# A decoder trunk on one core: the last tiles' transposes move into the first up product, the norm vectors into other tiles, and three groups of small work to other places in the queues

## The chip, the cores and the metric

One core of one Trainium2 chip runs the whole program; the other cores are idle. The metric is device microseconds from launch to the end, as the median of several runs. The profile is of one execution, and a span in it is the time from the first to the last instruction.

## What is computed

Two layers over 512 tokens of 1024 features, in float32. Layer 0 is a latent attention, layer 1 a banded one (window 128) whose keys and values come from the input of that layer. Each mixer and each MLP is followed by a scaled residual and a layer norm. Cut to what matters here:

```python
x = _layernorm(alpha * x + y, ln_mix_g[l], ln_mix_b[l])                    # y: the mixer
x = _layernorm(alpha * x + _mlp(x, mlp_w_up[l], mlp_w_down[l]), ln_mlp_g[l], ln_mlp_b[l])

def _mlp(x, w_up, w_down):          # 1024 -> 4096 -> 1024
    h = jax.nn.relu(x @ w_up)
    return (h * h) @ w_down
```

## The kernel before

**Numbers in two halves.** Every float32 operand is split into a rounded high part and the rest: ScalarE (ACT) writes the high part with a copy, VectorE (DVE) subtracts it (`split`, lines 75 to 83). A product is three matmuls, high by high, high by low and low by high (`three`). GpSimd (POOL) does the subtraction for some weights, and issues the adding DMAs.

**Tiles.** Tokens are in four tiles of 128 (t = 0 to 3). After a mixer, `TokMajor.finish` makes the second half of the output columns tile by tile, 24 matmuls of 512 columns for each t; as soon as a tile's group is in PSUM, DVE adds the residual (`add_scaled`, L541), takes the statistics (L534), and `layer_norm` (from L395) applies L400, L403 and L407, with a power on POOL (L384) between. `turn` then transposes the normed tile on TensorE (PE) through two PSUM banks of their own, and ACT and DVE split it into the operand of the next product. `finish` turns tile t-1 behind the groups of t = 1 and 2, so tiles 0 and 1; tiles 2 and 3 are turned later, by whoever comes next.

**MLP.** Up and down products are done with seven products in place of eight (U1 to U7 and D1 to D7, sums of quarter blocks). The order of the first ones is written out by hand: U1 U2 U5 U3 U6 U7 U4 D1 D2 (`FIRST_STEPS`). One U is four groups j = 0 to 3 of 12 matmuls of 256 columns. U1 and U2 need tiles 0 and 1 alone; U5 needs all four. U1 turns tile 2 behind its group j = 1, and U2 turns tile 3 behind its j = 1. D1 needs the factor f1, which is relu squared of the quarter a11, which is whole after U6; the quarters a21 and a22 are whole after U7 and U4.

**Weights** come from one stream in the order of use. `prep` of an entry issues the loading DMA on SP's queue, into one of two `raw` tiles (or a `wq` tile that later entries add to), and the split into one of four pairs of `wh` and `wl`. U1's and U2's four weights have places of their own (`w_fac`, `w_quada`, `w_quadb`, `w_a`). `hold` says up to which entry the stream may run ahead, and `prepare(n)` lets it run n further; `early`, the last argument of `finish`, says after which tile's norm it does.

**Band attention.** `begin` (from L560) makes keys and first queries in two halves of 256 tokens: chunks k0, k1 and sq0, each into a PSUM bank and evicted at once by 64-row copies (L1151, L1152, L1196, L1197); tile 2 is turned behind k1, tile 3 behind sq0.

**Order.** PE and SP run in program order. The other engines run in the order that the scheduler set when the program was built; `high_priority`, `pin` (program order) and `behind` / `issue_after` (an instruction may not stand ahead of a named one on its engine) steer it.

Of the kernel before, what the change touches and what calls it, by code (L numbers as in the profile page):

```python
# [15 lines left out]
P = 128  # L16
# [32 lines left out]
def build(tc, nc, io, out):  # L49
    with ExitStack() as top:  # L50
# [76 lines left out]
        def queue(name, ap, low=nc.vector):  # L127
# [24 lines left out]
            off_ring.append(False)  # L152
# [12 lines left out]
        def queue_seven(name, key, chunk):  # L165
# [88 lines left out]
        def mlp_stream(l):  # L254
            holds.append(len(stream) + 4)
# [22 lines left out]
        for m in range(2):  # L278
            queue("w_k", io["w_k"][m])
        for m in range(8):  # L280
# [109 lines left out]
        def load_gb(g, b):  # L390
            gb = gp.tile([P, 2, D], F32, tag="gb", bufs=1, name=nm("gb"))
            pe(nc.sync.dma_start(gb[:, 0, :], g.partition_broadcast(P)))
            pe(nc.sync.dma_start(gb[:, 1, :], b.partition_broadcast(P)))
            return gb

        def layer_norm(t, gb, dst):
# [6 lines left out]
            pin(nc.vector.scalar_tensor_tensor(x, x, mv[:, 0:1], gb[:, 0, :], ALU.subtract, ALU.mult))  # L403
            n = 2 if dst is None and t == NT - 1 else 1
            for i in range(n):
                c = slice(i * D // n, (i + 1) * D // n)
                pin(nc.vector.scalar_tensor_tensor(x[:, c], x[:, c], r, gb[:, 1, c], ALU.mult, ALU.add))  # L407
                if dst is None:
                    nc.sync.dma_start(out[t * P : (t + 1) * P, c], x[:, c])

        def turn_tokens(t, dst):

            tk = slice(t * P, (t + 1) * P)
            for n in range(2):
# [4 lines left out]
                split(dst.hs[n][:, :, tk], dst.ls[n][:, :, tk], pt)  # L419
# [140 lines left out]
        def begin(src, chunks):  # L560


            ws = [weights(name) for name, _ in chunks]
            for half_ in range(2):
                cols = slice(half_ * 256, half_ * 256 + 256)
                for i, (_, evac) in enumerate(chunks):
                    b = bank(256)
                    feat_major(src, ws[i], b, cols)
                    evac(cols, b)
                    if half_ == 0 and i > 0:  # L570
                        with tc.high_priority():
                            src.turn(i + 1)

# [86 lines left out]
        def mlp(src, gb, dst, mp):  # L660
# [17 lines left out]
            class Block:  # L678
# [18 lines left out]
                def up(self, n):  # L697
# [5 lines left out]
                    for j in range(4):  # L703
# [12 lines left out]
                        if (self.q, j) == (0, 1) and n in (1, 2):  # L716
                            with tc.high_priority():
                                src.turn(n + 1)

                def up_out(self, n, i):  # L720
# [7 lines left out]
                    elif n == 2:  # L728
                        nc.scalar.activation(self.quarter("a12")[:, pairs], of(1), AF.Relu)
                        if i == 1:  # L730
                            with behind(state.pop("s4") if self.q == 0 else None):
                                nc.scalar.activation(self.g["a12"], self.g["a12"], AF.Square)
# [18 lines left out]
                def factor(self, n, quad=False):  # L751
# [5 lines left out]
                    split(f[:, 0], f[:, 1], g[2] if n == 0 else self.down.sum(n, *g))  # L757
# [36 lines left out]
            for i, (which, q, n) in enumerate(steps):  # L794
                if which == "D":
# [3 lines left out]
                    at.setdefault(max(min(i - 2, i_last), i_q), []).append((q, n))  # L799
# [31 lines left out]
            TokMajor(Hidden(), add_last, "down").finish(gb, dst)  # L831
# [300 lines left out]
        gb = lambda: load_gb(io["ln_mix_g"][0], io["ln_mix_b"][0])  # L1132
        x2 = Feat()
        with tc.tile_pool(name="mlp0", bufs=1) as mp:
# [3 lines left out]
            proj.finish(gb, x1, (0, 0, 0, 2))  # L1138
            mlp(x1, lambda: load_gb(io["ln_mlp_g"][0], io["ln_mlp_b"][0]), x2, mp)
# [3 lines left out]
        with tc.tile_pool(name="swa", bufs=1) as mp:  # L1143
# [145 lines left out]
            for m in range(1, 8):  # L1289
                for part in range(2):  # L1290
                    fill.append((2.6, 2 * m - AHEAD_B - 3 + part, -9, lambda m=m, part=part: queries(m, part)))
                if m == 1:
# [4 lines left out]
            load_bias(0)  # L1297
# [3 lines left out]
                + [("w_sq", lambda cols, b: query_parts(0, cols, b))],  # L1301
# [4 lines left out]
        gb = lambda: load_gb(io["ln_mix_g"][1], io["ln_mix_b"][1])  # L1306
        with tc.tile_pool(name="mlp1", bufs=1) as mp:
# [3 lines left out]
            proj.finish(gb, x3, (0, 0, 0, 2))  # L1311
            mlp(x3, lambda: load_gb(io["ln_mlp_g"][1], io["ln_mlp_b"][1]), None, mp)
# [109 lines left out]
```

## Time and profile before

| | us |
|---|---|
| median of 3 runs (lowest, highest) | 1033.54 (1028.98, 1035.62) |
| the profiled execution's own time | 1032.31 |
| its span | 1030.4 |
| PE busy in it | 998.7 (97%) |
| DVE, ACT, POOL busy | 769.6 (75%), 556.3 (54%), 218.5 (21%) |
| HBM traffic | 146 GB/s over the span |

A busy PE is read with care here: a matmul's row lasts longer than the distance to the next one, so what PE loses is read from the starts of successive matmuls, not from the busy share. Times in the prediction are microseconds from the start of the span.

### The profile page before, as it was taken

How to read it: one execution, taken by the hardware profiler on the slowest of the kernel's cores; microseconds unless marked ns; L12 is line 12 of the kernel's file. 1: busy time of each engine (PE TensorE's matmuls, PEld its weight loads, DVE VectorE, ACT ScalarE, POOL GpSimd, SP SyncE). 2: the span in 40 equal slices, each digit the busy share in tenths (PEclk: the TensorE clock that was granted, in tenths of full speed). 3: DMA queues.
4: the chain of work that ended last, by engine and by line, in shares of the span. 5: the costliest groups of instructions: out<-in, count | busy, mean ns of one | idle time of the engine just before them, and what ended most of it. 6: DMA issues, size and time to landing. Idle time of an engine off the chain costs nothing.

```text
span 1030.4 us, 15886 instructions
## 1 busy us (share of the span) xinstructions
PE 998.7 (97%) x6148; PEld 897.6 (87%) x6148; DVE 769.6 (75%) x1233; ACT 556.3 (54%) x849; POOL 218.5 (21%) x204
## 2 busy tenths in 40 slices
PE   8999998998999999999999999989899999999997
PEld 8888887997999989998888888879798998988986
DVE  5588858788769769886685678778786796797756
ACT  5456643466637637646146689526654664565620
POOL 1232001112211211210004565122022122122000
PEclk9999999999999999999999999999899999999999
DMA  6421127289877987964132212349778788798432
GB/s 241 147 89 42 62 103 204 73 190 235 152 170 209 175 187 195 228 112 143 62 103 93 82 63 73 109 96 221 190 150 147 193 217 151 197 255 152 92 123 81
DMA packets 60246, 149.55 MB, mean 145 GB/s; under 512 B 5211, under 2 KB 9740, under 8 KB 60172
## 3 DMA queue, kind: packets, MB, share of 16 engines
q0 software_dynamic: 24320, 58.73, 32.3%
q1 hardware_dynamic: 35852, 89.82, 26.0%
q8 instruction: 48, 0.79, 0.3%
q14 instruction: 26, 0.21, 0.1%
HBM read 146.41 MB, written 4.22 MB: 146 GB/s over the span
## 4 chain that ended last, share of the span: by engine, by line
PE 82%; DMA 6%; DVE 5%; ACT 3%; issue 3%; POOL 0%; SPq 0%; DVEq 0%; ACTq 0%; POOLq 0%
PE mm L104 75%; PE tr L104 4%; DMA wq<-in_up 3%; ACT wh L77 1%; DMA raw<-in_w_o 1%; DMA raw<-in_up 1%; DVE wl L80 1%; PE tr L1083 1%; DMA raw<-in_w_so 1%; PE tr L630 1%; PE tr L1253 1%; DVE x L403 0%; DMA raw<-in_w_kv 0%; DVE bn L534 0%; DVE x L407 0%
## 5 line engine op out<-in xcount | busy, mean ns | idle before, releaser
L104 PE MATMUL mm<-wh,fac 128*128 128x512 f32 (+1 forms) x944 | 296.4, 391 | 6.2 <-ACT fac L77 4.9
L77 ACT ACTIVATE wh<-wq 128x1024 fp32r<-128x1024 f32 x164 | 173.3, 1060 | 194.2 <-PE mm L104 141.7
L80 DVE TENSOR_TENSOR wl<-wq,wh 128x1024 fp32r<-128x1024 f32 x164 | 199.6, 1221 | 80.4 <-ACT wh L77 79.3
L104 PE MATMUL mm<-xth,wh 128*128 128x256 f32 (+1 forms) x936 | 245.2, 290 | 3.1 <-DVE a L742 2.1
L104 PE MATMUL mm<-xth,wl 128*128 128x256 f32 (+1 forms) x808 | 234.6, 290 | 0.0
L104 PEld LDWEIGHTS mm<-wh,fac 128*128 128x128 f32 x944 | 178.1, 190 | 43.8 <-ACT fac L77 5.3
L104 PE MATMUL mm<-xtl,wh 128*128 128x256 f32 (+1 forms) x680 | 198.8, 292 | 1.2 <-DVE xtl L80 1.2
L104 PE MATMUL mm<-wl,fac 128*128 128x512 f32 (+1 forms) x472 | 184.1, 390 | 0.0
L104 PEld LDWEIGHTS mm<-xth,wh 128*128 128x128 f32 x936 | 170.1, 192 | 6.5 <-ACT wh L77 1.6
L104 PEld LDWEIGHTS mm<-xth,wl 128*128 128x128 f32 x808 | 154.7, 192 | 2.3
L77 ACT ACTIVATE wh<-raw 128x1024 fp32r<-128x1024 f32 (+4 forms) x85 | 84.8, 998 | 100.1 <-PE mm L104 64.4
L198 POOL DMA_DIRECT2D wq<-in_up x64 | 77.5, 1228 | 271.7 <-DVE wl L80 211.9
L104 PEld LDWEIGHTS mm<-xtl,wh 128*128 128x128 f32 x680 | 130.2, 192 | 4.4 <-DVE xtl L80 1.4
L80 DVE TENSOR_TENSOR wl<-raw,wh 128x1024 fp32r<-128x1024 f32 (+3 forms) x64 | 75.7, 1189 | 42.1 <-ACT wh L77 42.0
L104 PEld LDWEIGHTS mm<-wl,fac 128*128 128x128 f32 x472 | 89.9, 190 | 17.0
L198 POOL DMA_DIRECT2D wq<-in_down x48 | 42.0, 876 | 190.1 <-DVE wl L80 183.3
L80 POOL TENSOR_TENSOR wl<-raw,wh 128x1024 fp32r<-128x1024 f32 (+2 forms) x21 | 43.7, 2086 | 81.3 <-ACT wh L77 78.9
L104 PE MATMUL mm<-wh,oh 128*128 128x512 f32 x128 | 51.9, 405 | 0.9 <-ACT p L1233 0.9
L104 PE MATMUL mm<-wh,ol 128*128 128x512 f32 x128 | 50.9, 398 | 0.1
L104 PE MATMUL mm<-wl,oh 128*128 128x512 f32 x128 | 50.9, 397 | 0.0
L384 POOL TENSOR_TENSOR rs<-mv,half 128x1 f32<-128x1 f32 x16 | 9.9, 621 | 179.6 <-DVE mv L400 179.6
L544 DVE TENSOR_TENSOR x<-mm,x 128x512 f32<-128x512 f32 (+1 forms) x49 | 32.9, 675 | 15.0 <-PE mm L104 15.0
(217 smaller groups left out, 1845.9 us busy)
## 6 DMA issues: line engine op xcount, KB each, us to landing
wq<-in_up POOLq DMA_DIRECT2D x64, 512.0 KB, 7.9
wq<-in_down POOLq DMA_DIRECT2D x48, 512.0 KB, 6.6
wq<-in_up SPq DMA_DIRECT2D x32, 512.0 KB, 5.8
raw<-in_down SPq DMA_DIRECT2D x28, 512.0 KB, 6.5
wq<-in_down SPq DMA_DIRECT2D x24, 512.0 KB, 6.7
raw<-in_up SPq DMA_DIRECT2D x16, 512.0 KB, 5.4
raw<-in_w_o SPq DMA_DIRECT2D x8, 512.0 KB, 4.1
raw<-in_w_sq SPq DMA_DIRECT2D x8, 512.0 KB, 3.4
```

What stands on the lines that cost most here:

```text
L77: high = nc.scalar.activation(dst_h, src, AF.Copy)
L80: low = (engine or nc.vector).tensor_sub(dst_l, src, f32(dst_h))
L104: pe(nc.tensor.matmul(dst, st, mv, start=first and i == 0, stop=last and i == len(pairs) - 1, **kw))
L198: nc.gpsimd.dma_start(half(a, jp), chunk(*more, jp), accum_op=ALU.add)
L384: nc.gpsimd.tensor_tensor(r, v, half, ALU.pow)
L544: nc.vector.tensor_add(xs[t][:, c], b, xs[t][:, c])
L630: pe(nc.tensor.transpose(pt[:, a, :], xs[t][:, k * P : (k + 1) * P], ident))
L1083: pe(nc.tensor.transpose(pt[:, kb * P : (kb + 1) * P], p[:, kb * P : (kb + 1) * P], ident))
L1253: pe(nc.tensor.transpose(pt[:, a, 0:P], p[:, kb, P:256], ident))
```

## The change

The diff, without what only passes new arguments on:

```diff
         def queue(name, ap, low=nc.vector, after=False):
...
-                    state["plain"] = split(wh[:, c], wl[:, c], raw[:, c], low)
+                    with behind((state["norm"],) if after else None):
+                        state["plain"] = split(wh[:, c], wl[:, c], raw[:, c], low)
...
             def alone(jp, aside=None):
-                split(wh, wl, raw)
+                with behind(state.pop("f1", None) if key == "D" else None):
+                    split(wh, wl, raw)
...
         def mlp_stream(l):
-            holds.append(len(stream) + 4)
+            holds.append(len(stream) + 2)
...
         for m in range(8):
-            queue("w_sq", io["w_sq"][m], nc.gpsimd if m else nc.vector)
-            if m == 0:
+            queue("w_sq", io["w_sq"][m], nc.gpsimd if m > 1 else nc.vector, m < 2)
+            if m == 1:
                 for half_ in range(2):
                     queue("w_v", io["w_v"][half_])
...
+            if which == "mix":
+                gb = [mlp_pool[0].tile([P, D], F32, tag=tag, bufs=1, name=nm("gb")) for tag in ("a12", "a22")]
+            else:
+                both = gp.tile([P, 2, D], F32, tag="gb", bufs=1, name=nm("gb"))
+                gb = [both[:, 0, :], both[:, 1, :]]
...
         def begin(src, chunks):
+            state["hold"] = len(stream)
             ws = [weights(name) for name, _ in chunks]
+            late = []
...
                     feat_major(src, ws[i], b, cols)
-                    evac(cols, b)
-                    if half_ == 0 and i > 0:
+                    late.append((evac, cols, b))
+                    if half_ == 0 and i in (1, 2):
                         with tc.high_priority():
                             src.turn(i + 1)
+                    if half_ or i > 2:
+                        with behind(src.last if not half_ else None):
+                            for evac, *at in late:
+                                evac(*at)
+                        late = []
...
-                        if (self.q, j) == (0, 1) and n in (1, 2):
+                        if (self.q, n) == (0, 1) and j in (0, 3):
                             with tc.high_priority():
-                                src.turn(n + 1)
+                                src.turn(NT - 2 + j // 3)
...
-                        nc.scalar.activation(self.quarter("a12")[:, pairs], of(1), AF.Relu)
+                        with behind(state.pop("s4", None) if i == 1 else None):
+                            nc.scalar.activation(self.quarter("a12")[:, pairs], of(1), AF.Relu)
...
-                    at.setdefault(max(min(i - 2, i_last), i_q), []).append((q, n))
+                    at.setdefault(i_q if (q, n) == (0, 1) else max(min(i - 2, i_last), i_q), []).append((q, n))
...
-            TokMajor(Hidden(), add_last, "down").finish(gb, dst)
+            if dst is not None:
+                state["hold"] = first_sq
+            TokMajor(Hidden(), add_last, "down").finish(gb, dst, dst and (0, 0, 0, 1))
...
-            proj.finish(gb, x1, (0, 0, 0, 2))
+            proj.finish(gb, x1, (0, 2, 0, 2))
...
-            for m in range(1, 8):
+            for m in range(2, 8):
...
-                fill.append((0, u, u, lambda t=t, kp=kp: proj.part(t, kp)))
+                fill.append((1.3 if t < 2 else 0, u, u, lambda t=t, kp=kp: proj.part(t, kp)))
...
             begin(
                 x2,
                 [("w_k", lambda cols, b, m=m: keys(m, cols, b)) for m in range(2)]
-                + [("w_sq", lambda cols, b: query_parts(0, cols, b))],
+                + [("w_sq", lambda cols, b, m=m: query_parts(m, cols, b)) for m in range(2)],
             )
```

In words: (1) two of the four own weights of U1 and U2 are prepared after tile 1's norm and no longer ahead of tile 0's, in both layers; (2) the two vectors of a norm ahead of an MLP lie in the tiles of the quarters a12 and a22, and no longer in the tile that U3's weights use; (3) tile 2 is turned behind U1's group j = 0 and tile 3 behind its j = 3; (4) f1 is made right after U6, and D2's first weights stand behind it; (5) `begin` makes a fourth chunk sq1, whose queries were one product of 512 columns later on, evicts the first half's four banks only behind the split of tile 3, and the splits of sq0 and sq1 stand behind tile 3's norm. Rows on every engine up to the first norm are in the same order as before, and the matmuls of the MLPs and of the head loop stay as they are.

On DVE, at the end of layer 0's output projection (`x_1601` and `x_1603` are tiles 0 and 1, `x_1605` is tile 2, `mm` a PSUM bank), before:

```order
L80 TENSOR_TENSOR w_fac_1914<-wq_1912,w_fac_1914 128x1024
L80 TENSOR_TENSOR w_quada_1919<-wq_1912,w_quada_1919 128x1024
L538 TENSOR_SCALAR bn_1902<-bn_1902 128x1
L80 TENSOR_TENSOR w_quadb_1925<-raw_1923,w_quadb_1925 128x1024
L80 TENSOR_TENSOR w_a_415_1931<-raw_1928,w_a_414_1930 128x1024
L541 SCALAR_TENSOR_TENSOR x_1601<-x_1601,mm_1937 128x512
L534 BN_STATS bn_1872<-x_1601 128x6
L400 BN_AGGR mv_1964<-bn_1872 128x2
```

and now:

```order
L80 TENSOR_TENSOR w_fac_1914<-wq_1912,w_fac_1914 128x1024
L80 TENSOR_TENSOR w_quada_1919<-wq_1912,w_quada_1919 128x1024
L547 TENSOR_SCALAR bn_1902<-bn_1902 128x1
L550 SCALAR_TENSOR_TENSOR x_1601<-x_1601,mm_1927 128x512
L543 BN_STATS bn_1872<-x_1601 128x6
L408 BN_AGGR mv_1954<-bn_1872 128x2
```

```order
L411 SCALAR_TENSOR_TENSOR x_1603<-x_1603,mv_1987,gb_1923 128x1024
L415 SCALAR_TENSOR_TENSOR x_1603<-x_1603,rs_1989,gb_1924 128x1024
L80 TENSOR_TENSOR w_quadb_1995<-raw_1993,w_quadb_1995 128x1024
L80 TENSOR_TENSOR w_a_423_2001<-raw_1998,w_a_422_2000 128x1024
L550 SCALAR_TENSOR_TENSOR x_1605<-x_1605,mm_2023 128x512
```

The two splits moved from ahead of tile 0's first step to between tile 1's norm and tile 2's first step.

On ACT, before D1 of layer 0 (`a_479`/`a_480` is a11, `a_487`/`a_489` a21, `a_451`/`a_460` a12; `fac_2536`/`fac_2471` is f1; the two `wh<-raw` are D2's weights), before:

```order
L747 ACTIVATE a_479_2438<-a_479_2438 128x1024
L747 ACTIVATE a_487_2506<-a_487_2506 128x1024
L77 ACTIVATE wh_2547<-raw_2545 128x1024
L748 ACTIVATE a_479_2438<-a_479_2438 128x1024
L748 ACTIVATE a_487_2506<-a_487_2506 128x1024
L77 ACTIVATE wh_2609<-raw_2607 128x1024
L77 ACTIVATE fac_2536<-a_479_2438 128x1024
L77 ACTIVATE fac_2604<-a_451_2213 128x1024
```

and now:

```order
L764 ACTIVATE a_480_2439<-a_480_2439 128x1024
L764 ACTIVATE a_489_2510<-a_489_2510 128x1024
L765 ACTIVATE a_480_2439<-a_480_2439 128x1024
L765 ACTIVATE a_489_2510<-a_489_2510 128x1024
L77 ACTIVATE fac_2471<-a_480_2439 128x1024
L77 ACTIVATE wh_2548<-raw_2546 128x1024
L77 ACTIVATE fac_2605<-a_460_2250 128x1024
L77 ACTIVATE wh_2610<-raw_2608 128x1024
```

Two weight splits that stood ahead of f1 stand behind it. On DVE the same place (`a_495`/`a_496` is a22, whose second half reads U4's last bank), before and now:

```order
L745 TENSOR_TENSOR a_495_2575<-mm_2481,uv_2142 128x512
L80 TENSOR_TENSOR wl_2548<-raw_2545,wh_2547 128x1024
L745 TENSOR_TENSOR a_495_2575<-mm_2508,uv_2142 128x512
L80 TENSOR_TENSOR wl_2610<-raw_2607,wh_2609 128x1024
L80 TENSOR_TENSOR fac_2536<-a_479_2438,fac_2536 128x1024
```

```order
L762 TENSOR_TENSOR a_496_2576<-mm_2485,uv_2162 128x512
L762 TENSOR_TENSOR a_496_2576<-mm_2512,uv_2162 128x512
L80 TENSOR_TENSOR fac_2471<-a_480_2439,fac_2471 128x1024
L80 TENSOR_TENSOR wl_2549<-raw_2546,wh_2548 128x1024
L80 TENSOR_TENSOR fac_2605<-a_460_2250,fac_2605 128x1024
```

f1's low part comes one split earlier, but still behind both halves of a22.

On DVE, at the start of the band attention (`wl_4996`/`wl_5158` is sq0's low part, `wl_5185` sq1's; `xtl` tiles 2 and 3 after `turn`; `skl` and `q` are evictions), before:

```order
L80 TENSOR_TENSOR wl_4996<-raw_4994,wh_4995 128x1024
L400 BN_AGGR mv_5155<-bn_4972 128x2
L1152 TENSOR_TENSOR skl_5169<-mm_5198,skh_5165 64x256
L403 SCALAR_TENSOR_TENSOR x_1607<-x_1607,mv_5155,gb_4820 128x1024
L1152 TENSOR_TENSOR skl_5169<-mm_5198,skh_5165 64x256
L407 SCALAR_TENSOR_TENSOR x_1607<-x_1607,rs_5157,gb_4820 128x1024
L80 TENSOR_TENSOR wl_5182<-raw_5180,wh_5181 128x1024
L1152 TENSOR_TENSOR skl_5171<-mm_5231,skh_5167 64x256
L80 TENSOR_TENSOR xtl_1829<-tr_5264,xth_1827 128x4x128
```

and now:

```order
L408 BN_AGGR mv_5150<-bn_4973 128x2
L411 SCALAR_TENSOR_TENSOR x_1607<-x_1607,mv_5150,gb_4821 128x1024
L415 SCALAR_TENSOR_TENSOR x_1607<-x_1607,rs_5152,gb_4821 128x1024
L80 TENSOR_TENSOR wl_5158<-raw_5156,wh_5157 128x1024
L80 TENSOR_TENSOR wl_5185<-raw_5183,wh_5184 128x1024
L80 TENSOR_TENSOR xtl_1829<-tr_5257,xth_1827 128x4x128
```

The evictions and a weight moved out of tile 3's norm and from between the transposes' splits.

More of the change, by code (lines that the diff above doesn't have):

```diff
@@ L125, in raw_tile, with queue @@
             return wp.tile([P, 1024], F32, tag="raw", bufs=2, name=nm("raw"))
-        def queue(name, ap, low=nc.vector):
+        def queue(name, ap, low=nc.vector, after=False):
             index = len(stream)
@@ L388, in build, with load_gb @@
         xs = [None] * NT
[L390 to L393, printed above, removed]
+        def load_gb(which, l):
+            if which == "mix":
[3 more added lines that the diff above has]
+                gb = [both[:, 0, :], both[:, 1, :]]
+            for to, of in zip(gb, "gb"):
+                pe(nc.sync.dma_start(to, io[f"ln_{which}_{of}"][l].partition_broadcast(P)))
             return gb
@@ L418, in turn_tokens @@
                     pe(nc.tensor.transpose(pt[:, a, :], xs[t][:, k * P : (k + 1) * P], ident))
-                split(dst.hs[n][:, :, tk], dst.ls[n][:, :, tk], pt)
+                dst.last = split(dst.hs[n][:, :, tk], dst.ls[n][:, :, tk], pt)
         class Pair:
@@ L728, in up_out @@
                     elif n == 2:
-                        nc.scalar.activation(self.quarter("a12")[:, pairs], of(1), AF.Relu)
+                        with behind(state.pop("s4", None) if i == 1 else None):
+                            nc.scalar.activation(self.quarter("a12")[:, pairs], of(1), AF.Relu)
                         if i == 1:
-                            with behind(state.pop("s4") if self.q == 0 else None):
-                                nc.scalar.activation(self.g["a12"], self.g["a12"], AF.Square)
+                            nc.scalar.activation(self.g["a12"], self.g["a12"], AF.Square)
                     elif n == 6:
@@ L756, in factor @@
                     g = [self.g.get(a) for a in ("a11", "a12", "a21", "a22")]
-                    split(f[:, 0], f[:, 1], g[2] if n == 0 else self.down.sum(n, *g))
+                    pair = split(f[:, 0], f[:, 1], g[2] if n == 0 else self.down.sum(n, *g))
+                    if (self.q, n) == (0, 1):
+                        state["f1"] = pair
                     self.fac[n] = f
@@ L1295, in build @@
             for t, kp, u in ((0, 0, 11), (0, 1, 11), (1, 0, 13), (1, 1, 14), (2, 0, 14), (2, 1, 15), (0, 2, 15), (1, 2, 16)):
[L1296 to L1297 removed]
+                fill.append((1.3 if t < 2 else 0, u, u, lambda t=t, kp=kp: proj.part(t, kp)))
+            for m in range(2):
+                load_bias(m)
             begin(
```

18 lines of the change are left out of this document (10 added, 8 removed).

## The prediction

> **What bounds the kernel now.** I read the page's chain of waits first: PE is 82% of the chain that ends last, and nothing else reaches a tenth.
>
> ```profile
> PE 82%; DMA 6%; DVE 5%; ACT 3%; issue 3%; POOL 0%; SPq 0%; DVEq 0%; ACTq 0%; POOLq 0%
> ```
>
> So the program is a queue of matmuls, and time is won only where PE stands still, runs at a lower clock, or gets fewer matmuls. The waits of PE come next; the columns are the total, the times and the longest. The change touches the places behind these five:
>
> ```profile
> PE tr L630 <- DVE x L407: 5.9, 2, 3.1
> PE mm L104 <- ACT fac L77: 4.9, 2, 2.4
> PE mm L104 <- DVE a L742: 2.1, 2, 1.4
> ...
> PE mm L104 <- DVE q L1197: 1.7, 1, 1.7
> ...
> PE mm L104 <- DVE fac L80: 1.3, 2, 0.7
> ```
>
> All but q come twice, once a layer. A wait shows less than the loss, so I measure the loss by the starts of successive matmuls, less the distance that they have undisturbed. The PE timeline gives both, here at layer 0's norm:
>
> ```profile
> 175.81 0.39 PE L104 MATMUL mm<-wl,oh 128*128 128x512 f32 x1
> 176.04 0.39 PE L104 MATMUL mm<-wh,ol 128*128 128x512 f32 x1
> 179.15 1.09 PE L630 MATMUL tr<-ident,x 128*128 128x128 f32 x8 [2.72 <-DVE x L407]
> ```
>
> The undisturbed distance is 0.23 at 512 columns, so the transposes were due at 176.27 and came 2.88 late, 0.16 more than the wait. Layer 1's wait is 3.1 by the list, so I take 3.3. Third, the windows, for the clock. Columns: length, busy time (count) of PE, PEld, DVE, ACT and POOL, then granted clock, DMA share, GB/s.
>
> ```profile
> 180.30:183.60 3.30, 3.30 (x9) 2.55 (x8) 3.14 (x6) 1.82 (x4) 0.56 (x1) 0.50 0.01 2
> ...
> 238.30:241.60 3.30, 1.70 (x6) 1.14 (x7) 3.30 (x3) 3.27 (x4) 0.00 (x0) 1.00 0.87 245
> 241.70:245.00 3.30, 3.30 (x9) 2.61 (x8) 1.74 (x3) 1.47 (x2) 0.00 (x0) 0.50 0.80 212
> ...
> 678.60:681.90 3.30, 3.09 (x12) 2.80 (x13) 2.71 (x6) 1.68 (x3) 0.42 (x1) 0.50 0.35 65
> ...
> 740.10:746.80 6.70, 6.09 (x15) 4.57 (x15) 5.15 (x6) 3.38 (x4) 0.00 (x0) 0.50 0.86 309
> ```
>
> Directly after each of the four longest stalls (at the norm and at D1, in both layers) PE runs at half clock: three stretches of 3.4 (1.7 lost in each) and one of 6.8 (about 2.9 lost, since part of it was waiting anyway). These 8.0 us stand in no list of waits.
>
> **Part 1: two weights behind tile 1's norm.** DVE at layer 0's norm:
>
> ```profile
> 171.31 1.22 DVE L80 TENSOR_TENSOR w_quadb<-raw,w_quadb 128x1024 fp32r<-128x1024 f32 x1
> ...
> 173.56 1.22 DVE L80 TENSOR_TENSOR w_a<-raw,w_a 128x1024 fp32r<-128x1024 f32 x1 [1.04 <-ACT w_a L77]
> 174.70 0.68 DVE L541 SCALAR_TENSOR_TENSOR x<-x,mm 128x512 f32<-128x512 f32 x1
> ...
> 177.81 1.28 DVE L407 SCALAR_TENSOR_TENSOR x<-x,rs,gb 128x1024 f32<-128x1024 f32 x1
> ```
>
> Tile 0's chain takes 4.39 (174.70 to 179.09). Without the two splits it starts at 171.31 and ends at 175.70, ahead of 176.27: the stall goes. What is late next? The tile groups are 24 matmuls, 24 x 0.23 = 5.5, and a tile's eight transposes 0.8 (rows below). Group 1 ends at 176.3; tile 1's chain, started some 0.6 later because the last matmul must drain, ends at 181.3 to 181.8. Its turn is due at 176.3 + 0.8 + 5.5 = 182.6. Then the two splits, 2.4, hold DVE until 184.2, past the end of group 2 (182.6), and tile 2's chain ends at 188.6 to 189.6.
>
> **Part 3: the turns inside U1** make that enough. U1 can start at 182.6 + 0.8 + 5.5 = 188.9; tile 2's turn, behind j = 0 (12 x 0.12 = 1.4), is due at 190.3, and tile 3's, behind three more groups and the transposes, at 195.4, when its chain ends at about 194.5. The margins are 0.7 to 1. U5, which needs all four tiles, is due at 188.9 + 1.6 + 11.5 (U1 and U2, 96 x 0.12) = 202; tile 3 is turned by 196.2, which leaves 5.8 for its splits and sums. I leave 0.2 per layer for the thinnest. Gain: 2.88 + 3.3, less 0.4, and the half clock behind them, 2 x 1.7.
>
> **Part 2: the norm vectors in a12 and a22** take their two loads on SP ahead of the weights' loads, not behind them; they are read at 172 and 173.6 in the new order, and their issue is ahead of that. U3's weights no longer wait for the old tile to be free, so they come earlier, under U1 and U2, where PE waits for nothing. I cost it at nothing: cover is the whole of U1 and U2, 96 matmuls (11.5 us). If that cover were gone, a late weight would cost PE its lateness once a layer. Between a gain of nothing and a loss of 1.7, the wait ACT has for a load of this stream today, I take nothing:
>
> ```profile
> 172.47 1.06 ACT L77 ACTIVATE w_a<-raw 128x1024 fp32r<-128x1024 f32 x1 [1.71 <-DMA raw<-in_up]
> ```
>
> **Part 4: f1 before D2's weights.** PE in layer 0, ahead of U4's last products and at D1:
>
> ```profile
> 229.73 0.28 PE L104 MATMUL mm<-xtl,wh 128*128 128x256 f32 x1
> 229.85 0.28 PE L104 MATMUL mm<-xth,wl 128*128 128x256 f32 x1
> 230.76 0.47 PE L104 MATMUL mm<-xth,wh 128*128 128x256 f32 x2 [0.63 <-DVE a L742]
> ...
> 236.46 0.28 PE L104 MATMUL mm<-xth,wl 128*128 128x256 f32 x1
> 239.18 0.50 PE L104 MATMUL mm<-wh,fac 128*128 128x512 f32 x1 [2.44 <-ACT fac L77]
> 239.52 0.40 PE L104 MATMUL mm<-wl,fac 128*128 128x512 f32 x1
> 240.63 0.73 PE L104 MATMUL mm<-wh,fac 128*128 128x512 f32 x2 [0.72 <-DVE fac L80]
> ```
>
> Losses: 0.79 before U4 (0.91 less 0.12), 2.60 for f1's high part, 0.88 for its low part; 4.27. In layer 1 the first is 1.4 + 0.16 by the list; 5.05. What f1 is made of, on ACT and DVE:
>
> ```profile
> 230.05 1.06 ACT L77 ACTIVATE wh<-wq 128x1024 fp32r<-128x1024 f32 x1 [1.54 <-PE mm L104]
> ...
> 235.25 1.99 ACT L748 ACTIVATE a<-a 128x1024 f32<-128x1024 f32 x2
> 237.14 1.04 ACT L77 ACTIVATE wh<-raw 128x1024 fp32r<-128x1024 f32 x1
> 238.09 1.99 ACT L77 ACTIVATE fac<-a 128x1024 fp32r<-128x1024 f32 x2
> 236.78 0.69 DVE L745 TENSOR_TENSOR a<-mm,uv 128x512 f32<-128x512 f32 x1 [0.18 <-PE mm L104]
> 239.36 2.35 DVE L80 TENSOR_TENSOR fac<-a,fac 128x1024 fp32r<-128x1024 f32 x2
> ```
>
> U7 ends at 229.97 (229.85 and one distance). ACT's split at 230.05 is U4's last weight, which waits for U7 to free its place; it ends 1.14 after U7 and stays ahead. Behind it ACT now has the relus of a11 and a21, their squares and f1's high part in one row, five of about 1.0 (half of 1.99), without the two weight splits of 1.04: f1 is there 6.0 after U7's end. D1 is due U4's 48 x 0.12 = 5.76 after it. The high part costs 0.2 to 0.45. The low part still stands on DVE behind a22's second half (236.78), which reads U4's last bank: 0.2 + 0.69 + 1.2 (half of 2.35) = 2.1 after U4's end. D1's first two matmuls, 0.45, need the high part alone, so high and low together cost 1.65, where they cost 3.48. The wait ahead of U4 I take as gone, since U3's earlier loads leave room on the queue in which U4's came, and DVE's reads of U7's banks, for which U4 waits, come earlier with them (ends: 0 and the 0.79 of today). So 1.65 of 4.27 and of 5.05 stay. The clock: in the window from 238.30 above, PE stood for 1.6 of 3.3, and the next was at half. 1.65 of standing is at that edge, and falls across two windows as likely as into one; I count half a drop, 0.85 per layer (ends: none and 1.7).
>
> **Part 5: begin.** PE, before:
>
> ```profile
> 528.68 1.04 PE L418 MATMUL tr<-ident,x 128*128 128x128 f32 x8
> 529.47 0.36 PE L104 MATMUL mm<-xth,wh 128*128 128x256 f32 x1
> ...
> 532.30 0.28 PE L104 MATMUL mm<-xth,wl 128*128 128x256 f32 x1
> ...
> 533.08 0.66 PE L418 MATMUL tr<-ident,x 128*128 128x128 f32 x4 [0.51 <-DVE xtl L80]
> 534.26 0.66 PE L418 MATMUL tr<-ident,x 128*128 128x128 f32 x4 [0.52 <-DVE xtl L80]
> 534.68 0.36 PE L104 MATMUL mm<-xth,wh 128*128 128x256 f32 x1
> 536.23 0.39 PE L104 MATMUL mm<-xtl,wh 128*128 128x256 f32 x1 [1.19 <-DVE xtl L80]
> ```
>
> Eight transposes take 0.79. From 532.30 to 536.23 are 3.93, with eight of them and two matmuls: 2.90 lost, because DVE makes tile 3's split behind evictions and a weight. Now sq1's 24 matmuls, 2.9 us, stand between the turn of tile 3 and the first product that needs it, and the evictions behind the split. Those are four groups of this size, three in all:
>
> ```profile
> 543.45 1.74 DVE L1152 TENSOR_TENSOR skl<-mm,skh 64x256 fp32r<-64x256 f32 x4 [1.47 <-ACT skh L1151]
> ```
>
> that is 3 x 1.74 = 5.2, ending near 540, when the second half's third chunk needs a bank near 542. ACT takes sq1's high split in order and may wait for its load: 0.5 left (ends 0 and 2.9). The wait for q, 1.7 in the list (1.86 start to start), goes because the evictions ahead of it are done two products earlier. Work: 48 matmuls of 256 more, 24 of 512 fewer, 5.76 against 5.45: 0.3 lost.
>
> **The sum.** Stalls 6.2 + 9.3 + 2.9 + 1.8, clock 8.0: 28.2 aimed at. Left over or new: 0.4 (norms), 3.3 (D1), 1.7 (clock at D1), 0.5 and 0.3 (begin): 6.2. Gain 22. The profiled execution took 1032.3, the median is 1033.5 (1.2 higher, and the runs lie 6.6 apart): 1010.3 or 1011.5, and I say 1011.
>
> [...]
>
> **Rivals.**
>
> *The norms' gain is given back at D1 (0.10).* PE comes 4.6 us earlier per layer, and if DVE and ACT then set the pace through U1 to U4, PE waits for f1 instead. For it: DVE is busy 3.3 of 3.3 before D1. Against: f1's row on ACT starts at U7's end, whenever that is, and no backlog feeds it. All of it leaves begin's 3.9 alone, 1029 or 1030; half of the rest, 1020.
>
> *The half clocks stay (0.08).* They come at the same places without the stalls, from another cause: for it, the one at 740.10 lasts 6.8, though by the list of waits the stall ahead of it was no longer than that at 236.46; against, the first window after each of the four stalls has it. The gain loses 8.0 less the 1.7 counted: 1017. [...]
>
> *Begin brings nothing (0.06).* ACT waits for sq1's load with tile 2's split queued behind it, and DVE's evictions come late for the banks. For it: a wait of 1.71 for such a load, above. Against: PE has four chunks of 2.9 ahead of it, in which a load of this size can land. 2.4 + 1.8 less: 1015.
>
> *Slower (0.04).* w_quadb's and w_a's splits stand on DVE between tile 1's norm and tile 2's first step, and their loads now stand behind the vectors' two on SP. Each microsecond that they land after 182 holds DVE, then turns 2 and 3, then U1 and U5. It decides from some 12 us late in each layer, which eats the 22 with the margins of 0.7; 18 us late make 1046. For it: ACT waited 1.71 for w_a's load. Against: that load was there at 172.5, and has 9 us more.
>
> *It does not do what it says (0.02)*, the scheduler having undone it: 1033. The rows of the order speak against it.
>
> **How the numbers follow.** My forecast has 0.70; its own range is the sum with each unknown at its ends: 1005 (nothing left over) to 1019 (D1's clock full 1.7, begin 2.4 more, U4's wait 1.6, norms 1 late each). The two rivals at 1015 and 1017 lie in it; the first takes it to 1022. Below, the spread of the runs adds some: 1003 to 1022 leaves about 0.15 out, nearly all of it above. A measurement of this kernel tells about 1% from no change, 10 us. Faster by more: the forecast, the clock, begin and half of the first rival, 0.89, of which I take 0.01 off for the unforeseen, 0.88; within 1%: the rest of the first rival and no effect, 0.08; slower by more 0.04.
>
> **What would show it.** PE's waits on x (L407) at L630 gone or under 0.5; half clocks only near D1, two at most; waits for f1 of about 0.4 (ACT) and 1.2 (DVE) a layer; no wait for q; U1 4.5 us earlier. It is wrong if a wait on DVE of over 1 us stands at the turns in U1, if more than 3 us a layer stay at D1, or if PE's new order waits for weights.

## The result and the profile after

The changed kernel took 1009.28 us (median of 4 runs, 1007.26 to 1009.88) beside 1034.25 of the kernel before (4 runs, 1028.98 to 1035.62): a ratio of 0.9766, 95% interval 0.9734 to 0.9798. In a later group it was 0.9783 (0.9764 to 0.9801). The profiled execution took 1009.88 with a span of 1008.0: 22.4 less span than before.

The waits of PE in the changed kernel (total, times, longest):

```profile
PE mm L104 <- DVE fac L80: 2.3, 2, 1.2
PE mm L104 <- ACT p L1255: 1.6, 6, 0.7
PE mm L104 <- POOL zeros L343: 1.4, 1, 1.4
PE mm L104 <- DVE wl L80: 1.1, 2, 0.8
PE mm L104 <- DVE o L1305: 0.8, 1, 0.8
```

Of the four largest rows of before, the first three are gone, and so are q's and those of begin's turns. The fourth, p, is still there (L1233 then, L1255 now): 2.0 in two waits then, 1.6 in six now. The third and fourth rows above are of the first 13 us. What the places lost, by the starts of successive matmuls less their undisturbed distance:

| | before | forecast to stay | after |
|---|---|---|---|
| the two norms | 6.2 | 0.4 | 0 |
| ahead of U4 and at D1, both layers | 9.3 | 3.3 | 3.0 |
| begin, and the wait for q | 4.8 | 0.5 | 0 |
| half clock | 8.0 | 1.7 (at D1) | 1.7 (in the head loop) |
| head loop of the band attention | 2.9 | not touched | 3.5 |
| work added | | 0.3 | 0.3 |
| sum | 31.2 | 9.1 | 8.5 |

The forecast's sum takes the head loop at its old 2.9, the three waits of over 0.5 that it had. The table gives 22.7, and the span fell by 22.4. The start of the program makes part of the difference: a matmul that waits for ql in layer 0's attention, ahead of all five changes, starts at 102.16 before and at 102.78 after; PE's waits for the first weights cost 2.5 there, and 1.7 before. From that matmul to the end the gain is 23.0.

**The norm.** PE and then DVE, layer 0 (rs is the power on POOL):

```profile
176.57 0.39 PE L104 MATMUL mm<-wh,ol 128*128 128x512 f32 x1
176.80 1.03 PE L647 MATMUL tr<-ident,x 128*128 128x128 f32 x8
```

```profile
171.84 0.68 DVE L550 SCALAR_TENSOR_TENSOR x<-x,mm 128x512 f32<-128x512 f32 x1
...
175.28 1.29 DVE L415 SCALAR_TENSOR_TENSOR x<-x,rs,gb 128x1024 f32<-128x1024 f32 x1 [0.44 <-POOL rs L387]
...
182.18 1.22 DVE L80 TENSOR_TENSOR w_quadb<-raw,w_quadb 128x1024 fp32r<-128x1024 f32 x1
183.31 1.22 DVE L80 TENSOR_TENSOR w_a<-raw,w_a 128x1024 fp32r<-128x1024 f32 x1
184.45 0.68 DVE L550 SCALAR_TENSOR_TENSOR x<-x,mm 128x512 f32<-128x512 f32 x1
```

The transposes follow the last matmul by 0.23, as if nothing stood between. The chain on DVE started at 171.84 where 171.31 was forecast, lost 0.44 to POOL, and ended at 176.57: 0.23 ahead of PE. The two splits run where they were forecast, 182.2 to 184.5.

**D1.** PE and DVE, layer 0; layer 1 shows the same:

```profile
231.39 0.28 PE L104 MATMUL mm<-xth,wl 128*128 128x256 f32 x1
231.68 0.50 PE L104 MATMUL mm<-wh,fac 128*128 128x512 f32 x1
232.02 0.40 PE L104 MATMUL mm<-wl,fac 128*128 128x512 f32 x1
233.58 0.73 PE L104 MATMUL mm<-wh,fac 128*128 128x512 f32 x2 [1.17 <-DVE fac L80]
```

```profile
231.71 0.69 DVE L762 TENSOR_TENSOR a<-mm,uv 128x512 f32<-128x512 f32 x1 [2.19 <-PE mm L104]
232.31 1.22 DVE L80 TENSOR_TENSOR fac<-a,fac 128x1024 fp32r<-128x1024 f32 x1
```

The high part costs 0.17 (231.68 for 231.51), the low part 1.34 (1.56 less 0.23): DVE stood idle for 2.19 and then made a22 first and f1's low part second. Together 1.51, where 1.65 was forecast. No half clock follows. Here is the window that holds layer 1's wait (columns as in the prediction: length, PE busy first, granted clock third from the end); the one after it is at 1.00 too:

```profile
719.96:723.37 3.41, 2.24 (x10) 1.70 (x10) 3.41 (x4) 3.38 (x5) 0.00 (x0) 1.00 0.55 108
```

**Begin.** PE turns tile 3 without a wait, and the first half's evictions are done at 530.96:

```profile
523.79 1.11 PE L427 MATMUL tr<-ident,x 128*128 128x128 f32 x8
```

```profile
525.06 1.29 DVE L80 TENSOR_TENSOR xtl<-tr,xth 128x512 fp32r<-128x512 f32 x2 [0.87 <-ACT xth L77]
526.26 0.74 DVE L1174 TENSOR_TENSOR skl<-mm,skh 64x256 fp32r<-64x256 f32 x2
...
530.20 0.76 DVE L1174 TENSOR_TENSOR skl<-mm,skh 64x256 fp32r<-64x256 f32 x2
```

**The head loop** is where the only wait with a half-clock window behind it now stands:

```profile
616.67 0.50 PE L104 MATMUL mm<-wh,oh 128*128 128x512 f32 x1 [0.18 <-ACT p L1255]
625.31 0.39 PE L104 MATMUL mm<-skh,q 128*128 128x256 f32 x1 [0.83 <-DVE o L1305]
626.74 0.50 PE L104 MATMUL mm<-wh,oh 128*128 128x512 f32 x1 [0.69 <-ACT p L1255]
```

### The profile page after: what moved, and what is told of

Read it like the earlier page. It is cut to its first block, busy times and chain, and to the rows that moved or that the text cites. A ratio compares the mean times of both kernels' runs of the same rounds, so it can differ in the third digit from the quotient of the medians.

```text
span 1008.0 us, 15943 instructions
## 1 busy us (share of the span) xinstructions
PE 991.8 (98%) x6172; PEld 895.1 (89%) x6172; DVE 770.6 (76%) x1236; ACT 555.0 (55%) x851; POOL 216.1 (21%) x203
## 4 chain that ended last, share of the span: by engine, by line
PE 95%; ACT 2%; DVE 1%; DMA 1%; issue 1%; SPq 0%; DVEq 0%; ACTq 0%
PE mm L104 87%; PE tr L104 5%; DMA xraw<-in_xT 1%; PE tr L1105 1%; PE tr L647 1%; ACT p L1255 1%; ACT wh L77 1%; PE tr L1275 1%; PE tr L1277 0%; PE tr L427 0%; ACT q L1218 0%; DVE fac L80 0%; ACT pth L77 0%; PE mm L1035 0%; PE tr L899 0%
## 5 line engine op out<-in xcount | busy, mean ns | idle before, releaser
L104 PE MATMUL mm<-wh,fac 128*128 128x512 f32 (+1 forms) x944 | 293.0, 387 | 2.4 <-DVE fac L80 2.3
L80 POOL TENSOR_TENSOR wl<-raw,wh 128x1024 fp32r<-128x1024 f32 (+2 forms) x20 | 41.4, 2075 | 86.4 <-ACT wh L77 83.9
```

Source lines behind the costliest of these rows:

```text
L80: low = (engine or nc.vector).tensor_sub(dst_l, src, f32(dst_h))
L104: pe(nc.tensor.matmul(dst, st, mv, start=first and i == 0, stop=last and i == len(pairs) - 1, **kw))
```

## The experiments

Five kernels undo one part each, the other parts kept; two take away a wait that was left; one measures the clock; a last group repeats what mattered on one chip. Ratios are to the kernel before, run in the same group (the changed kernel's is 0.9766 and 0.9783). The groups ran on different chips (the kernel before has medians of 1034.25, 1030.84, 1029.28 and 1030.98 in them), so a single microsecond is read from the traces and not from medians.

### Part 1 undone

```diff
-            holds.append(len(stream) + 2)
+            holds.append(len(stream) + 4)
...
-            proj.finish(gb, x1, (0, 2, 0, 2))
+            proj.finish(gb, x1, (0, 0, 0, 2))
```

(the last line likewise for layer 1)

> The changed kernel with part 1 alone undone: the splits of w_quadb and w_a stand ahead of tile 0's first step again, in both layers; all else as changed. My theory (a stall is lost time, and the half clock follows the stall): PE's wait for x at the first turn comes back, 2.9 and 3.3 us, and the window after each is at half clock, 1.7 each: 9.6 more than the changed kernel's 1009.3, so about 1019. [...] Rival B (the norm is not what bounds this place, PE would wait at U5 or D1 instead): 1009 to 1011.

1017.42 us, ratio 0.9865 (0.9843 to 0.9887): some 8 to 10 us slower than the changed kernel. PE at the first turn of layer 0 (the view ends after five of its eight transposes), and what DVE does before it:

```profile
175.34 0.39 PE L104 MATMUL mm<-wh,ol 128*128 128x512 f32 x1
179.47 0.77 PE L647 MATMUL tr<-ident,x 128*128 128x128 f32 x5 [3.75 <-DVE x L415]
```

```profile
173.89 1.23 DVE L80 TENSOR_TENSOR w_a<-raw,w_a 128x1024 fp32r<-128x1024 f32 x1 [1.98 <-ACT w_a L77]
175.03 0.68 DVE L550 SCALAR_TENSOR_TENSOR x<-x,mm 128x512 f32<-128x512 f32 x1
```

3.91 in layer 0 and 3.62 in layer 1, each followed by a half-clock window: PE's rows were busy for 0.79 and 0.90 us of the windows of 3.41 ahead (from 176.85 and 668.37), and the clock granted over the span is 0.995, where the changed kernel's second trace has 0.998. Both were larger than in the kernel before, since w_a's split waits 1.98 for ACT where it waited 1.04. Rival B falls: PE does not wait at U5 or D1 instead.

### Part 3 undone

```diff
-                        if (self.q, n) == (0, 1) and j in (0, 3):
+                        if (self.q, j) == (0, 1) and n in (1, 2):
...
-                                src.turn(NT - 2 + j // 3)
+                                src.turn(n + 1)
```

(with a12's relu and square ordered as before)

> The changed kernel with part 3 alone undone: tile 2 is turned behind U1's j = 1, tile 3 behind U2's j = 1, as before. My theory (the operand of U5 hangs on tile 3's turn, and in the changed kernel it is there 0.84 us before U5): the turn comes 3.6 us later, so U5 waits 0.7 to 2.5 us in each layer; at the lower end without half clock, 1011, at the upper with it, 1017. Rival (the place of the turns does not matter, since part 1 already made room): 1009, no wait at U5.

1013.01 us, ratio 0.9829 (0.9806 to 0.9851). The time lies in the expected range, and the place was wrong: no wait stands at U5. PE's waits:

```profile
PE mm L104 <- DVE fac L80: 1.3, 2, 0.6
PE mm L104 <- DVE a L759: 1.2, 2, 0.6
PE mm L104 <- ACT fac L77: 1.1, 2, 0.5
```

U4 waits again for DVE to read U7's banks (L759): 0.78 and 0.74 by the starts; D1 loses 1.5 a layer as in the changed kernel. The span is 1009.2, where the changed kernel's second trace has 1006.1: 3.1 more. Of this, 0.7 lies ahead of 102 us, where this execution has a half-clock window (9.06 to 12.47) and that one has none; the clocks granted over the spans are 0.997 and 0.998. From there on it is 2.4, of which U4's two waits are 1.5 and a wait of 0.35 for a copy (L795) in layer 1's D2 is another part; neither trace has a half clock there but at the very end. So the early turns serve, as far as this run shows, not U5's operand but what DVE has to do between there and U4. I had read U5's slack of 0.84 as a path from the turn; but the operand's high part stood behind a copy on ACT that waited for PE, so with a later turn the way from turn to operand shrank from 5.0 to 3.1.

### Part 4 undone

```diff
-                    at.setdefault(i_q if (q, n) == (0, 1) else max(min(i - 2, i_last), i_q), []).append((q, n))
+                    at.setdefault(max(min(i - 2, i_last), i_q), []).append((q, n))
...
-                with behind(state.pop("f1", None) if key == "D" else None):
+                with behind(None):
```

> The changed kernel with part 4 alone undone: f1 is made where it was, and D2's first two weights are split ahead of it. My theory: the two stalls at D1 are 2.6 and 0.9 again where they are now 1.34 together, so 2.1 more in each layer, and a half-clock window behind each, 1.7: 7.7 more, 1017. Rival A (no half clock from stalls of this length): 1013.5. Rival B (f1 is early enough anyhow since the loads come earlier): 1009 to 1010.

1012.92 us, ratio 0.9827 (0.9808 to 0.9847). PE in layer 0:

```profile
232.92 0.50 PE L104 MATMUL mm<-wh,fac 128*128 128x512 f32 x1 [1.11 <-ACT fac L77]
234.18 0.73 PE L104 MATMUL mm<-wh,fac 128*128 128x512 f32 x2 [0.53 <-DVE fac L80]
...
243.47 0.50 PE L104 MATMUL mm<-wh,fac 128*128 128x512 f32 x1 [1.30 <-DVE u L795]
```

By the starts 1.27, 0.70 and 1.46, the third inside D2, on a copy (L795) that DVE makes late: 3.43, and 3.45 in layer 1, where the changed kernel loses 1.51. The sum, 1.9 a layer, is near the expected 2.1, its place is not: at D1 itself 1.97, against 3.48 before, so other parts had already taken 1.5 off. And there is no half clock (the windows from 235.67 and 723.76, behind D1's waits, are at 1.00, and the clock over the span is 0.998), so of the expected 7.7 the two waits' 3.9 are left.

### Part 5 undone

`begin` and its callers as before, with three chunks and the product of 512 columns for sq1's queries:

```diff
-                    late.append((evac, cols, b))
-                    if half_ == 0 and i in (1, 2):
+                    evac(cols, b)
+                    if half_ == 0 and i > 0:
...
-            for m in range(2, 8):
+            for m in range(1, 8):
```

> The changed kernel with part 5 alone undone: three chunks at the start of the band attention, evicted at once, sq1 as one product of 512 columns. My theory: 2.9 at the turn of tile 3 and 1.9 at q come back, 0.3 of work goes: 4.5 more, 1013.8; the waits at the end of the head loop (3.5 and a half-clock window of 1.7 in the changed kernel's profile) may fall to the 3.1 of before without a half clock, which would give 1011.7. Rival (part 5 brought nothing, it only moved the waits into the head loop): 1009 to 1010.

1011.61 us, ratio 0.9816 (0.9792 to 0.9839). The old waits are back: 2.75 at the turn of tile 3, counted as the prediction counts the 2.90 (526.80 less 523.02, less eight transposes and two matmuls), and 1.86 at q:

```profile
524.85 0.66 PE L427 MATMUL tr<-ident,x 128*128 128x128 f32 x4 [0.53 <-DVE xtl L80]
526.80 0.39 PE L104 MATMUL mm<-xtl,wh 128*128 128x256 f32 x1 [1.18 <-DVE xtl L80]
...
547.51 0.33 PE L104 MATMUL mm<-skh,q 128*128 128x128 f32 x1 [1.70 <-DVE q L1209]
```

and the head loop falls to 1.64 (0.58 and 1.06), without the five waits of 0.34. So part 5 takes 4.6 of waits away, gives 1.9 back in the head loop and adds 0.3 of work: about 2.4, not the 3.9 of the forecast. The rival is right for 1.9 of the 4.6. The kernel before had one wait more in the loop, 1.24 at 595.40, behind a wait of 2.22 on ACT for a load of w_so. It is in no later trace, here neither, so part 5 is not what took it away; what did is open.

### Part 2 undone

```diff
-            if which == "mix":
+            if False:
```

> The changed kernel with part 2 alone undone: the norm vectors ahead of the MLPs lie in the tile that U3's weights use; the order on every engine stays, only U3's loads wait for the tile. My costing put part 2 itself at nothing and gave the end of U4's wait (0.8 and 1.6) to the earlier loads. Theory A (the earlier loads ended U4's wait): the wait for DVE ahead of U4 comes back, 0.8 to 2.4 in all, 1010 to 1012. Theory B (the loads have time anyhow): 1009, no new wait. Theory C (the norms' vectors are what matter, PE or DVE waits for the tile at U3): over 1013.

1012.34 us, ratio 0.9826 (0.9793 to 0.9859). The order of the instructions is the changed kernel's on every engine, so only the loads differ. PE ahead of U4, and a weight on ACT some 7 us before:

```profile
227.10 0.48 PE L104 MATMUL mm<-xth,wh 128*128 128x256 f32 x2 [1.59 <-DVE a L759]
```

```profile
220.52 1.06 ACT L77 ACTIVATE wh<-wq 128x1024 fp32r<-128x1024 f32 x1 [1.84 <-DMA wq<-in_up]
```

In the changed kernel the same split stands at 218.41, 2.1 earlier. U4 waits 1.75 and 1.33 by the starts, 3.1 in all; D1 loses its 1.5 as before. Theory A holds. What was costed at nothing in its own place takes U4's wait away, which stands some 36 us after the start of U1.

### f1 in one row on ACT

```diff
+                        with behind(state.pop("f1_high", None) if n == 7 else None):
-                        nc.scalar.activation(self.g[done], self.g[done], AF.Relu)
+                            nc.scalar.activation(self.g[done], self.g[done], AF.Relu)
...
                         state["f1"] = pair
+                        state["f1_high"] = pair[:1]
```

> The changed kernel with one edit more: ACT's relu of a21 may not stand ahead of f1's high part, so that relu, square and f1 of a11 come in one row. Theory (the 1.34 left at D1 is f1's low part, which stands behind the relu and square of a21 on ACT and behind a22's second half on DVE): f1 comes 1.9 us earlier, both its parts are there before D1, 1.34 goes in each layer: 1006.6. Rival (a21 becomes late and the sums for D5 make PE wait instead): 1009 or above, with a wait at D5 or D2.

1005.1 us, ratio 0.9759 (0.9733 to 0.9785), and once more in the last group, below: 1003.73. From that trace ACT, DVE and PE at D1:

```profile
225.49 1.06 ACT L765 ACTIVATE a<-a 128x1024 f32<-128x1024 f32 x1
226.58 1.06 ACT L766 ACTIVATE a<-a 128x1024 f32<-128x1024 f32 x1
227.67 1.06 ACT L77 ACTIVATE fac<-a 128x1024 fp32r<-128x1024 f32 x1
```

```profile
228.76 1.23 DVE L80 TENSOR_TENSOR fac<-a,fac 128x1024 fp32r<-128x1024 f32 x1 [0.73 <-ACT fac L77]
230.22 0.69 DVE L762 TENSOR_TENSOR a<-mm,uv 128x512 f32<-128x512 f32 x1 [0.23 <-PE mm L104]
```

```profile
229.90 0.28 PE L104 MATMUL mm<-xth,wl 128*128 128x256 f32 x1
230.02 0.40 PE L104 MATMUL mm<-wh,fac 128*128 128x512 f32 x1
230.25 0.40 PE L104 MATMUL mm<-wl,fac 128*128 128x512 f32 x1
230.49 0.62 PE L104 MATMUL mm<-wh,fac 128*128 128x512 f32 x2
```

f1's low part is made in the 2.2 us in which DVE had stood idle, and PE goes from U4 into D1 at its undisturbed distance, in both layers. a21, now later, makes nobody wait in either trace of this kernel. The theory holds.

### The clock, by two stalls of one size

```diff
+                            for _ in range(2 if t == 0 and early == (0, 2, 0, 2) else 0):
+                                pin(nc.vector.scalar_tensor_tensor(xs[t], xs[t], 1.0, xs[t], ALU.mult, ALU.max))
                             layer_norm(t, gb, dst)
```

> The changed kernel with two more operations on DVE ahead of tile 0's norm in each layer (each gives x back as it was, some 1.2 us), so that PE waits about 2.2 us at the first turn in layer 0 and 1.9 in layer 1. It measures the clock alone. Theory (a window of the 3.4 us grid in which PE stands for more than about 1.5 us is followed by one at half clock): a half-clock window behind a stall in most executions, depending on how the grid cuts it; 4.1 of stalls and 0 to 3.4 of clock, 1013.4 to 1016.8. [...]

1015.14 us, ratio 0.9854 (0.9828 to 0.9881). PE waited 2.25 at the turn in layer 0 and 2.19 in layer 1, and only the second was followed by half clock. Half-clock stretches of one trace begin whole multiples of 3.413 us apart (in the kernel before 18, 128 and 18 of them, last section), so they give the grid. Its windows here around the first stall and then the second (length, PE busy first, granted clock third from the end):

```profile
174.83:178.24 3.41, 1.90 (x9) 1.24 (x7) 2.91 (x4) 0.68 (x1) 1.66 (x1) 1.00 1.05 226
178.24:181.66 3.42, 2.84 (x17) 2.50 (x18) 3.35 (x6) 1.68 (x3) 0.55 (x1) 1.00 0.99 180
...
666.35:669.76 3.41, 1.38 (x11) 1.01 (x10) 2.92 (x4) 0.69 (x2) 1.03 (x1) 1.00 1.11 226
669.76:673.18 3.42, 3.42 (x10) 2.64 (x10) 3.27 (x6) 1.97 (x4) 0.56 (x1) 0.50 0.65 119
```

The grid cut the first stall into two windows and left the second whole. PE was busy for 1.38 us of the 3.41 ahead of the half clock. This trace has one half-clock window more, behind the head loop (from 628.80; 1.90 busy in the window ahead), as the changed kernel's first trace has.

### One product a head later

```diff
-            for t, kp, u in ((0, 0, 11), (0, 1, 11), (1, 0, 13),
+            for t, kp, u in ((0, 0, 11), (0, 1, 12), (1, 0, 13),
```

> The changed kernel with one product of six matmuls in the head loop moved a head later, so that it stands between the scores of the last two heads. Theory (the two waits of 0.98 and 0.85 at 624 to 627 are PE two heads ahead of DVE and ACT, and the half-clock window behind them is theirs): the first goes, the second shrinks, PE stands for under 1.3 in a window and the half clock goes: 1.3 to 1.8 and 1.7 less, 1006 to 1007.5. Rival (DVE and ACT bound the whole loop, the wait only moves): 1009.

1008.38 us, ratio 0.9794 (0.9768 to 0.982): no gain that the times show. The wait moved:

```profile
620.01 0.30 PE L1275 MATMUL tr<-ident,p 128*128 128x128 f32 x1 [0.60 <-DVE ptl L80]
627.17 0.50 PE L104 MATMUL mm<-wh,oh 128*128 128x512 f32 x1 [0.71 <-ACT p L1255]
```

0.78 and 0.86 by the starts, where 0.98 and 0.85 stood. The theory falls: the wait only moves, as the rival has it. That DVE and ACT bound the whole loop, the rival's reason, is not shown by it.

### The last group, on one chip

> The changed kernel itself, once more beside the kernel before, as the measure for the other two of this group. 0.976 to 0.978 of the time of before; the half clock in the head loop in some executions only, since the grid of 3.4 us falls differently in each.

> The changed kernel with f1 of a11 in one row ahead of a21's relu, as in the earlier run of this edit, now beside the changed kernel on the same chip. The two waits of 1.34 at D1 gone: 2.7 less, and a little more where a half clock goes by chance; if the earlier gain was the chip's, within 1 us of the changed kernel.

> Both edits that took waits away: f1 of a11 in one row, and the product of six matmuls one head later. 2.7 for the first and 1.1 for the second less than the changed kernel's, and no half clock behind the head loop's end (the wait there is cut into 0.8 and 0.9 in two windows), 0.4 to 1.7 more: 1003.5 to 1005 where the changed kernel takes 1009. Rival (the second edit only moves the wait and the clock does not care): as the first edit alone.

| | us, median | ratio (95%) |
|---|---|---|
| the changed kernel | 1007.91 (5 runs) | 0.9783 (0.9764 to 0.9801) |
| f1 in one row | 1003.73 (4 runs) | 0.9747 (0.9724 to 0.977) |
| f1 in one row, and one product a head later | 1004.14 (4 runs) | 0.9741 (0.9724 to 0.9758) |

f1 in one row is 4.2 by the medians, though the two intervals overlap at their ends. The waits taken away are 3.0. The two traces differ by 4.7 in span (1006.1 and 1001.4), but 1.1 of that lies ahead of 102 us, which the edit does not touch; from there on it is 3.6, so 0.6 has no wait to its name. The second edit brings nothing beside it. The version to keep is f1 in one row alone.

This group also shows one reason why the changed kernel's own times differ. Here are the same two waits of the head loop, 0.98 and 0.85, on the grid of two executions: first the changed kernel's first trace, then its second.

```profile
624.38:627.79 3.41, 1.89 (x10) 1.42 (x10) 3.18 (x10) 3.36 (x13) 1.82 (x2) 1.00 0.01 2
627.79:631.20 3.41, 3.41 (x16) 3.12 (x15) 1.89 (x9) 2.07 (x6) 2.73 (x3) 0.50 0.00 0
```

```profile
622.22:625.63 3.41, 2.59 (x22) 2.29 (x19) 2.90 (x15) 3.31 (x10) 1.53 (x2) 1.00 0.01 2
625.63:629.05 3.42, 2.73 (x18) 2.31 (x17) 2.87 (x12) 2.88 (x11) 1.19 (x2) 1.00 0.00 0
```

Both waits in one window, half clock, span 1008.0; one in each, none, span 1006.1.

## Why the prediction was right, and where its steps were not

- **The sum.** 22 was forecast and 22.4 measured between the two profiled spans; by the medians it is 25.0 in the first group and 23.1 in the last. Three terms were off (the clock at D1, begin and the head loop, the half clock behind it), and they nearly cancel. That is luck: the half clock in the head loop, which the prediction did not have, stands in the first trace for the one counted at D1. The second trace, with a span of 1006.1, has neither.
- **The norms** (left over 0.4): nothing stayed. Undoing part 1 brings 3.9 and 3.6 back, and PE has no other wait that would take their place. The 0.6 that the prediction puts between a group's end and DVE's start on its tile is not in the traces: it was 0.20 (187.37 for 187.17 in the kernel before, 177.00 for 176.80 now). That PE would give the gain back at D1, the first rival, did not happen in any run.
- **D1** (1.65 a layer left): 1.34 by the low part and 0.17 by the high part's start, together 1.51, from the cause named, f1's low part behind a22. Moving it ahead removed it.
- **The clock at D1** (half a drop a layer, 1.7): the step that failed in size. Neither profiled execution of the changed kernel has one there. The estimate compared two counts: 1.65 is standing by the starts, and the 1.6 of 3.3 in the window from 238.30 is standing by the rows, which last longer (0.39 us at 512 columns, where the starts are 0.23 apart). By the starts PE stood there for 2.05 of 3.41 (window from 238.25), and in the changed kernel's windows at D1 for 1.58 and 1.47, less than the 2.0 in the window from 624.38, the shortest standing that half clock followed in the first traces of the two kernels.
- **The U4 wait** (taken as gone): it is gone, by part 2's loads, as said. But the prediction put it to the loads alone, and undoing the turns brings 0.78 and 0.74 back too, where 0.79 and 1.58 stood before. Why DVE is late there without the early turns was not tried by itself.
- **Part 3** was explained wrongly: the turns do not make part 1 hold and U5 had no wait without them.
- **Begin** (0.5 left, 3.9 won with the work): nothing stayed at its place, but some 1.9 came back in the head loop, which the prediction took as untouched. PE's work in the loop fell by one product of 24 matmuls, and five waits of 0.34 came up. That ACT and DVE set the pace of a head there, and so PE waits, is read from the name of these waits (ACT p, L1255) and is not shown by a run.
- **The half clock** (8.0, and a rival that it stays): it went with the stalls and came back with them, in part 1 undone, and behind the one of the two added stalls that the grid left whole. In the kernel before, PE's rows were busy for 1.07, 1.76, 0.52 and 0.97 us of the windows of 3.41 ahead of the four stretches.
- **The slower rival** (weights' splits late between tile 1 and tile 2) did not come near: the loads were there, and the splits ran back to back at 182.18 and 183.31.

## What to carry to other kernels

Add to a stall the half clock that follows it (up to 1.7 us for each window of 3.41 here), and ask of each small stall whether it falls with another into one window of the grid. Where a wait is undone far from the edit, look for the loads: an edit that is worth nothing in its own place can be worth 3 us where its queue is used next. And before leaving a late operand as a residue, look for the idle time of the engine that makes it: DVE stood for 2.2 us right before the wait of 1.34 that it caused.

## What the runs showed of the hardware

In the kernel before, half-clock stretches begin at 180.22, 241.66, 678.57 and 740.01 us (three of 3.41, the fourth of 6.83) and at 1026.73, near the end: 18, 128, 18 and 84 times 3.413 apart. In the changed kernel's first trace they begin at 627.79 (3.41 long) and, near the end, at 1003.26: 110 times 3.413 apart. So they lie on a grid of 3.413 us in each of the two.

These are windows of the grid, all at full clock, with the time for which PE's rows were busy in each, and the clock of the next window:

| window from | trace | PE busy of 3.41 | next window |
|---|---|---|---|
| 675.15 | before | 0.52 | half |
| 736.59 | before | 0.97 | half |
| 176.81 | before | 1.07 | half |
| 666.35 | the two added stalls | 1.38 | half |
| 238.25 | before | 1.76 | half |
| 624.38 | changed, first trace | 1.89 | half |
| 625.39 | the two added stalls | 1.90 | half |
| 174.83 | the two added stalls | 1.90 | full |
| 234.83 | before | 1.91 | full |
| 720.35 | part 4 undone | 2.00 | full |
| 531.79 | before | 2.22 | full |
| 719.96 | changed, first trace | 2.24 | full |
| 231.85 | changed, first trace | 2.25 | full |
| 622.22 | changed, second trace | 2.59 | full |

At 1.90 both stand, so the rows do not part them. The starts do, in the two traces counted. Give each matmul its undisturbed distance from its start on (0.227 us at 512 columns, 0.174 at 384, 0.147 at 320, 0.120 at 256, 0.067 at 128, and 0.100 for a transpose), and add up what falls into a window. In the traces of the kernel before and of the changed kernel (its first), from the first full clock to the end, half clock followed each of the seven full-clock windows with up to 1.42 us of such work (the one from 1023.31 of the kernel before has none), and none of the other 578, of which the least has 1.54 (from 531.79, before). These figures are of the two traces alone; the count was found afterwards, and no run was made to try it.

Two short waits counted together as one long one in the window from 624.38 (1.89 busy, or 1.42 by the starts). The grid lay differently to the same waits in the two traces of the changed kernel, with windows from 624.38 and from 622.22, and they cost 1.7 us more in the one and nothing more in the other. The kernel before has four stalls with half clock behind them and varied by 6.6 us in its first group; the changed kernel has this one place and varied by 2.6. That the grid is the whole of this variation was not tried.
